# Gate and up products with the tokens as stationary operand, their result turned by block transposes and DMAs of quarters

## The chip, the cores and the metric

The kernel runs on one core of a Trainium2 chip. The core has a matrix engine (TensorE, PE in the profile; its loads of the stationary operand are PEld), a vector engine (VectorE, DVE), a scalar engine (ScalarE, ACT), a general engine (GpSimd, POOL) and a queue engine (SyncE, SP) that issues DMAs. Each engine works through its own list of instructions in order and waits on semaphores for the others. The metric is the device time of one execution in microseconds (us), as the median of several.

## The reference

The reference is two transformer blocks over 256 tokens of width 2048 in fp32. The first is a sliding-window attention block with attention sinks. The second has two attention branches (latent attention and differential attention), merged by gates, and then a feed-forward part. Only the feed-forward part and the last norm are touched here:

```
x  = x + merged @ w_out
h2 = rmsnorm(x, ffn_norm_g)
x  = x + (silu(h2 @ w_ffn_gate) * (h2 @ w_ffn_up)) @ w_ffn_down      # D_FF = 5632
return rmsnorm(x, final_norm_g)
```

## The kernel before

**Weights.** All weight matrices are cut into tiles of 128 x 128 and laid out in the order in which the kernel uses them: 5440 tiles in 340 *chunks* of 16 tiles (1 MB each). Class `Weights` streams them. `load` (L53) issues one DMA on SP for a chunk into one of four buffers `w_raw`. `cut` (L84, L85) splits half a chunk (8 tiles) into a high part `w_hi`, rounded on ScalarE, and a low part `w_lo`, the remainder on VectorE; four buffers each, so two chunks in split form. `take` hands out the tiles. Activations are split in the same way, and a product is hi*hi + hi*lo + lo*hi, accumulated in fp32 in PSUM.

**Two forms of matmul.** In `gemm` (L319, through `run`, L296) the weight tile is stationary and the tokens stream past: for each tile one matmul of 512 columns (the tokens' high and low parts side by side) and one of 256 columns. The result has features in the partitions and tokens along the free axis, which is the form that the next matrix needs as input. In `gemm_nat` (L375, through `nat3`, L367) the tokens are stationary, two blocks of 128, and four weight tiles side by side stream past: for each of the two blocks three matmuls of 512 columns. The result has tokens in the partitions. `down` uses `gemm_nat` (L989), gate and up use `gemm` (L963, L966; `gemm4` for the first two pairs).

**Feed-forward.** Gate and up are 1408 tiles, chunks 208 to 295; down is chunks 296 to 339. For each of 44 blocks of 128 features (L958 to L971) a gate and an up product are made; `total` (L389, L201) adds the two halves of a PSUM bank, `scaled` multiplies by the broadcast row `rb` of the norm's factor, Silu is applied (L965), the two are multiplied, and `split_scaled` (L234, L235) writes the split result `act`, which down takes. The residual `x2` lies with features in the partitions; the generator `after_out` (L939), of which `Interleave` puts one step among the matmuls after every 16 tiles, turns it with 32 transposes on TensorE (L949) and copies them out (L952) as `x2n`, tokens in the partitions, for the last residual addition (`residual`, L981).

**Order.** The program is written in Python in one order; a scheduler then sets the order of each engine's list, by its own estimate of when operands are ready, and every engine keeps to that list. A DMA of SP also waits, beside its data, for the eighth DMA before it on SP: eight semaphores are used in turn. A load of chunk c waits until chunk c - 4 is split, and a split of a half waits until the half four before it has been used by TensorE.

Of the kernel before, what the change touches and what calls it, by code (L numbers as in the profile page):

```python
# [9 lines left out]
F32 = mybir.dt.float32  # L10
# [160 lines left out]
def block_kernel(ctx, tc, order, w, x01, xt, bc, fg, cst, out):  # L171
# [247 lines left out]
    def transposed(p, on_act=False):  # L419
# [7 lines left out]
        else:  # L427
            nc.vector.tensor_copy(out=pt, in_=ps[:, 0:384])
        return pt


# [494 lines left out]
    for m, ps in blocks("out", 0, 16, mg):  # L926
# [7 lines left out]
        sq.add(t)  # L934
    rb = unit("rb_3")[:, 0:S]
    r_3 = const.tile([P, 2], F32, name="r_3")
    x2n = []

    def after_out():  # L939
        yield  # L940
        nc.vector.tensor_copy(out=r_3, in_=rstd(sq.sums(), D))
        yield
        rows(r_3, rb)
        for cb in range(4):
            for tb in range(2):
                yield
                ps = bank("t")
# [4 lines left out]
                nc.scalar.copy(out=t, in_=ps)  # L952
# [105 lines left out]


def _columns(v):  # L1060
    return np.asarray(v, np.float32).reshape(-1, P).T


def _matrices(i):

    pairs = []
    for j in range(16):
# [7 lines left out]
    kpe = in_2[:, 1280:1344]  # L1075
    ffn = np.concatenate([i["w_ffn_gate_2"][0], i["w_ffn_up_2"][0]], axis=1)
    return {
# [13 lines left out]
        "ffn": ffn,  # L1091
        "down": i["w_ffn_down_2"][0],
    }
# [34 lines left out]
```

## Time and profile before

| | |
|---|---|
| median of 3 runs | 2022.9 us (2022.58 to 2024.06) |
| the profiled execution | 2023.11 us |
| its span, first to last instruction | 2021.3 us |
| instructions in the span | 28390 |
| moved by DMAs | 364.83 MB, mean 180 GB/s |
| gate and up on TensorE | 1278.9 to 1773.3 us of the span |
| down on TensorE | 1773.3 us to the end of the matmuls |

A profile gives, for each engine, the instructions with their start and length. The *page* sums them. *Groups* put instructions of one line, engine and shape together; *by tile* does so for those that touch one named buffer; *waits* says which engine waited for which instruction; the *chain that ended last* is followed back from the last instruction, each step to what released it; the *timeline* lists instructions by start; *windows* sum a stretch of time. L198 is the line of the matmul helper and L201 that of the two-operand VectorE helper, so these are told apart by their buffers.

### The profile page before, as it was taken

The numbers are of one execution on the slowest core, as the hardware profiler recorded it, in microseconds if no ns is written. First come the engines' busy times: TensorE is split into PE (matmuls) and PEld (weight loads), VectorE is DVE, ScalarE is ACT, GpSimd is POOL, SyncE is SP. The second block draws the span as 40 slices with busy tenths as digits, with TensorE's granted clock in tenths as the row PEclk, the third lists the DMA queues.
The fourth block names the chain that finished last, engine by engine and source line by source line (L and its number), as shares of the span: only waits on it lengthen the run. The fifth ranks groups of instructions, "written<-read, shape, count | busy, mean of one in ns | idle before, by whom it ended". The sixth has DMA issues, their size and how long they took to land.

```text
span 2021.3 us, 28390 instructions
## 1 busy us (share of the span) xinstructions
PE 2007.7 (99%) x11338; PEld 1744.3 (86%) x11338; DVE 1309.4 (65%) x2151; ACT 1074.6 (53%) x1821; POOL 18.4 (1%) x25
## 2 busy tenths in 40 slices
PE   9999999999999999999999999999999999999998
PEld 8888888888888888888888888888888888888887
DVE  7778766887857555576665667656666666554544
ACT  6677665756546444455565445554444445444443
POOL 0000000000000000000000000000000000000000
PEclk9999999999999999999999999999999999999999
DMA  8444454444344555545445555455555555555553
GB/s 300 152 144 149 165 209 176 167 149 155 135 169 167 188 188 188 190 167 186 172 166 188 192 196 190 175 179 187 189 188 189 192 191 191 194 209 189 196 197 104
DMA packets 53235, 364.83 MB, mean 180 GB/s; under 512 B 6064, under 2 KB 6576, under 8 KB 9968
## 3 DMA queue, kind: packets, MB, share of 16 engines
q1 hardware_dynamic: 51552, 359.76, 49.8%
q10 hardware_dynamic: 1152, 1.97, 0.3%
q8 instruction: 88, 1.44, 0.3%
q0 software_dynamic: 400, 1.31, 0.2%
q14 instruction: 43, 0.35, 0.1%
HBM read 360.91 MB, written 2.10 MB: 180 GB/s over the span
## 4 chain that ended last, share of the span: by engine, by line
PE 96%; DVE 2%; ACT 1%; issue 1%; DMA 0%; POOL 0%; POOLq 0%; ACTq 0%
PE ps_g L198 88%; PE ps_s L198 5%; PE ps_t L198 2%; PE ps_t L423 1%; DVE rope_t L201 1%; DVE w_lo L85 0%; DVE k_n L201 0%; DVE q_r L201 0%; ACT w_hi L84 0%; DMA x01t<-x 0%; PE ps_t L949 0%; PE ps_t L853 0%; ACT prob L414 0%; PE ps_t L829 0%; DVE prob L408 0%
## 5 line engine op out<-in xcount | busy, mean ns | idle before, releaser
L85 DVE TENSOR_TENSOR w_lo<-w_raw,w_hi 128x1024 fp32r<-128x1024 f32 (+1 forms) x677 | 824.9, 1220 | 296.7 <-ACT w_hi L84 276.3
L84 ACT CAST w_hi<-w_raw 128x1024 fp32r<-128x1024 f32 (+1 forms) x677 | 708.2, 1047 | 352.9 <-PE ps_g L198 269.5
L198 PE MATMUL ps_g<-h,w_hi 128*128 128x512 f32 x3048 | 742.1, 392 | 0.1
L198 PEld LDWEIGHTS ps_g<-h,w_hi 128*128 128x128 f32 x3048 | 558.4, 188 | 111.2 <-issue 3.5
L198 PEld LDWEIGHTS ps_g<-h,w_lo 128*128 128x128 f32 x3048 | 392.1, 191 | 17.8 <-issue 3.2
L198 PE MATMUL ps_g<-h,w_lo 128*128 128x256 f32 x3048 | 404.0, 284 | 0.0
L198 PE MATMUL ps_g<-w_hi,act 128*128 128x512 f32 x688 | 212.1, 389 | 0.0
L198 PEld LDWEIGHTS ps_g<-w_hi,act 128*128 128x128 f32 x688 | 129.1, 188 | 26.9
L389 ACT COPY ffn<-ps_g 128x256 f32<-128x256 f32 x86 | 31.8, 373 | 200.6 <-PE ps_g L198 200.6
L198 PE MATMUL ps_g<-w_lo,act 128*128 128x512 f32 x344 | 133.8, 389 | 0.0
L201 DVE TENSOR_TENSOR ffn<-ffn,ps_g 128x256 f32<-128x256 f32 x86 | 35.8, 420 | 143.9 <-ACT ffn L389 143.9
L198 PE MATMUL ps_g<-w_hi,h 128*128 128x512 f32 x256 | 79.5, 389 | 0.0
L198 PEld LDWEIGHTS ps_g<-w_lo,act 128*128 128x128 f32 x344 | 64.6, 188 | 13.3
L198 PE MATMUL ps_g<-y_m,w_hi 128*128 128x512 f32 x256 | 63.8, 391 | 0.0
L198 PE MATMUL ps_g<-y_d,w_hi 128*128 128x512 f32 x256 | 61.2, 391 | 0.0
L198 PE MATMUL ps_g<-g,w_hi 128*128 128x512 f32 (+1 forms) x240 | 57.8, 377 | 0.0
L198 PEld LDWEIGHTS ps_g<-w_hi,h 128*128 128x128 f32 x256 | 48.0, 188 | 10.0
L198 PE MATMUL ps_g<-mg,w_hi 128*128 128x512 f32 x224 | 56.0, 391 | 0.0
L198 PEld LDWEIGHTS ps_g<-y_m,w_hi 128*128 128x128 f32 x256 | 47.0, 188 | 9.1
L198 PEld LDWEIGHTS ps_g<-y_d,w_hi 128*128 128x128 f32 x256 | 47.0, 188 | 9.1
L198 PE MATMUL ps_g<-c,w_hi 128*128 128x512 f32 x208 | 53.0, 397 | 0.0
L198 PE MATMUL ps_g<-w_lo,h 128*128 128x512 f32 x128 | 49.8, 389 | 0.0
(255 smaller groups left out, 1899.4 us busy)
## 6 DMA issues: line engine op xcount, KB each, us to landing
w_raw<-w SPq DMA_DIRECT2D x337, 1024.0 KB, 4.8
w_raw<-w SPq DMA_DIRECT2D x5, 512.0 KB, 7.6
x_t<-xt SPq DMA_DIRECT2D x7, 256.0 KB, 7.4
fgt<-fg POOLq DMA_DIRECT2D x4, 256.0 KB, 5.5
out<-x2n SPq DMA_DIRECT2D x4, 256.0 KB, 3.1
out<-x2n ACTq DMA_DIRECT2D x4, 256.0 KB, 3.5
x01t<-x SPq DMA_DIRECT2D x1, 310.0 KB, 4.8
w_raw<-w ACTq DMA_DIRECT2D x1, 256.0 KB, 5.0
```

The costliest lines, as they stand in the source:

```text
L84: a = nc.scalar.copy(out=hi[:, q], in_=src[:, q])
L85: b = nc.vector.tensor_tensor(out=lo[:, q], in0=src[:, q], in1=hi.bitcast(F32)[:, q], op=ALU.subtract)
L198: nc.tensor.matmul(out=o, lhsT=a, rhs=b, start=start, stop=stop, skip_group_check=True)
L201: nc.vector.tensor_tensor(out=o, in0=a, in1=b, op=op)
L389: nc.scalar.copy(out=o, in_=ps[:, S:])
L423: nc.tensor.transpose(out=ps[:, j * P:j * P + P], in_=p[:, j * P:j * P + P], identity=ident)
```

## The change

Gate and up are computed with `gemm_nat`, in 11 *units* of 512 features: four chunks of gate, then four of up. Unit u takes chunks 208 + 8u to 215 + 8u. Tokens lie in the partitions of the result, so the norm's factor `r_3` is a scale of the Silu on ScalarE, which reads PSUM, and VectorE multiplies the up product in PSUM by it. The row `rb` and the broadcasts are gone.

Down needs the product with features in the partitions. A block transpose on VectorE turns each 32 x 32 block of the 128 x 512 product in its place; the blocks are then moved to their partitions by 16 DMAs on SP, each of 32 partitions x 128 elements (16 KB, a *quarter*). ScalarE and VectorE split the result. x2 takes the same way: 32 transposes of 128 x 128 on VectorE and 8 x 16 quarters in place of the 32 transposes on TensorE and the copies, and the generator makes one of its eight steps in every third chunk and no longer in every one. The features that come together in this way are not in their old order, so the columns of gate, up and down and the final gain are permuted on the host beforehand and the output's columns afterwards.

```diff
     def nat3(o, hl, tb, hi, lo, first, last):
-        xh = hl[:, tb * P:tb * P + P]
-        xl = hl[:, S + tb * P:S + tb * P + P]
+        if isinstance(hl, list):
+            xh, xl = hl[tb]
+        else:
+            xh = hl[:, tb * P:tb * P + P]
+            xl = hl[:, S + tb * P:S + tb * P + P]
...
+    def moved(tr, name):
+        o = unit(name)
+        for a in range(4):
+            for b in range(4):
+                nc.sync.dma_start(out=o[32 * b:32 * b + 32, a * P:a * P + P],
+                                  in_=tr[32 * a:32 * a + 32, b * P:b * P + P])
+        return o
...
     def after_out():
         yield
         nc.vector.tensor_copy(out=r_3, in_=rstd(sq.sums(), D))
-        yield
-        rows(r_3, rb)
         for cb in range(4):
             for tb in range(2):
-                yield
-                ps = bank("t")
+                yield 3
+                tr = unit("x2_t")
                 for i in range(4):
-                    nc.tensor.transpose(out=ps[:, i * P:i * P + P], in_=x2[4 * cb + i][:, tb * P:tb * P + P],
-                                        identity=ident)
-                t = unit("x2n")
-                nc.scalar.copy(out=t, in_=ps)
-                x2n.append(t)
+                    nc.vector.transpose(
+                        out=tr.rearrange("p (a m j) -> p a m j", a=4, m=4)[:, :, i, :],
+                        in_=x2[4 * cb + i][:, tb * P:tb * P + P].rearrange("p (a j) -> p a j", a=4))
+                x2n.append(moved(tr, "x2n"))
...
-    for m in range(0, KF):
-        if m == 0:
-            b4 = gemm4("ffn", [0, KF, 1, KF + 1], h)
-        t = unit("ffn")
-        zg, zu = t[:, 0:S], t[:, S:]
-        ps = b4[2 * m] if m < 2 else gemm("ffn", m, h)
-        scaled(zg, ps, rb)
-        nc.scalar.activation(out=zg, in_=zg, func=AF.Silu)
-        ps = b4[2 * m + 1] if m < 2 else gemm("ffn", KF + m, h)
-        total(zu, ps)
-        tt(zu, zu, zg, ALU.mult)
-        hl = unit(f"act{m}", F32R)
-        split_scaled(zu, None, hl)
-        act.append(hl)
+    def hidden(pg, pu):
+        parts = []
+        for tb in range(2):
+            z = unit("ffn")
+            nc.scalar.activation(out=z, in_=pg[tb], func=AF.Silu, scale=r_3[:, tb:tb + 1])
+            parts.append(z)
+        yield
+        hls = []
+        for tb in range(2):
+            z = parts[tb]
+            tt(z, pu[tb], z, ALU.mult)
+            tr = unit("ffn_t")
+            nc.vector.transpose(out=tr, in_=z)
+            t = moved(tr, "ffn_m").rearrange("p (a g i) -> p g a i", a=4, g=4)
+            hi, lo = unit("act_hi", F32R), unit("act_lo", F32R)
+            nc.scalar.copy(out=hi.rearrange("p (g a i) -> p g a i", a=4, g=4), in_=t)
+            tt(lo.rearrange("p (g a i) -> p g a i", a=4, g=4), t,
+               hi.bitcast(F32).rearrange("p (g a i) -> p g a i", a=4, g=4), ALU.subtract)
+            hls.append((hi, lo))
...
+    for u in range(DFF // 512):
+        banks = []
+        work = hidden(gemm_nat("ffn", u * 512, h), banks)
+        next(work)
+        banks.extend(gemm_nat("ffn", DFF + u * 512, h))
+        for _ in work:
+            pass
```

The lists of the engines are the same as before up to the first matmul of gate. Three places in the feed-forward show what then moves. In the lists of the changed program L439 is a quarter, L958 a block transpose of x2, L972 the Silu, L980 the block transpose of a product and L983 the cast of `act_hi`; numbers behind a name tell buffers apart.

**SP, where unit 2 ends.** Before, the list from the last of the small loads to the end of the kernel:

```order
L460 DMA sinks<-bc 128x32
L53 DMA w_raw<-w 128x2048 x3
L461 DMA tab_a<-cst 128x384
L53 DMA w_raw<-w 128x2048 x333
L1033 DMA out<-x2n 128x512 x4
```

Now, from the load of chunk 231, the last of unit 2 (`w_raw_13363`), over those of chunks 232 and 233 to that of 234:

```order
L53 DMA w_raw_13363<-w 128x2048
L439 DMA x2n_13092<-x2_t_13087 32x128 x16
L439 DMA x2n_13216<-x2_t_13211 32x128 x16
L439 DMA x2n_13346<-x2_t_13341 32x128 x16
L439 DMA ffn_m_13400<-ffn_t_13398 32x128 x16
L53 DMA w_raw_13447<-w 128x2048
L53 DMA w_raw_13481<-w 128x2048
L439 DMA ffn_m_13424<-ffn_t_13422 32x128 x16
L53 DMA w_raw_13537<-w 128x2048
```

SP had nothing but loads for 333 DMAs; now 64 quarters stand between the loads of chunks 231 and 232, the last 16 of them those of unit 2's first product. In units 3 to 10 the quarters stand further back: behind the load of the fifth chunk after the unit's last, 16 of them, then two loads, then 16 more.

**VectorE, at the same place.** Before, ten rows from the feed-forward, where splits of weights (L85) and work on the products take turns:

```order
L85 TENSOR_TENSOR w_lo_13392<-w_raw_13389,w_hi_13391 128x1024
L201 TENSOR_TENSOR ffn_13243<-ffn_13243,ps_g_13291 128x256
L201 TENSOR_TENSOR ffn_13243<-ffn_13243 128x256
L85 TENSOR_TENSOR w_lo_13396<-w_raw_13389,w_hi_13395 128x1024
L235 TENSOR_TENSOR act9_13337<-ffn_13243,act9_13337 128x256
L85 TENSOR_TENSOR w_lo_13442<-w_raw_13439,w_hi_13441 128x1024
L201 TENSOR_TENSOR ffn_13340<-ffn_13340,ps_g_13341 128x256
L201 TENSOR_TENSOR ffn_13340<-ffn_13340,rb_3_12298 128x256
L85 TENSOR_TENSOR w_lo_13446<-w_raw_13439,w_hi_13445 128x1024
L85 TENSOR_TENSOR w_lo_13489<-w_raw_13486,w_hi_13488 128x1024
```

Now, from the split of chunk 231's second half (`w_lo_13382`) to that of chunk 232's first (`w_lo_13450`):

```order
L85 TENSOR_TENSOR w_lo_13382<-w_raw_13363,w_hi_13381 128x1024
L958 STREAM_TRANSPOSE x2_t_13341<-y_2857 128x4x32 x2
L958 STREAM_TRANSPOSE x2_t_13341<-y_2858 128x4x32 x2
L201 TENSOR_TENSOR ffn_13233<-ps_g_13237,ffn_13233 128x512
L201 TENSOR_TENSOR ffn_13235<-ps_g_13238,ffn_13235 128x512
L980 STREAM_TRANSPOSE ffn_t_13398<-ffn_13233 128x512
L201 TENSOR_TENSOR act_lo_13418<-ffn_m_13400,act_hi_13417 128x512
L980 STREAM_TRANSPOSE ffn_t_13422<-ffn_13235 128x512
L85 TENSOR_TENSOR w_lo_13450<-w_raw_13447,w_hi_13449 128x1024
```

Unit 2's products, both transpositions and the subtraction, which needs all sixteen quarters of `ffn_m_13400`, now stand ahead of the first split of chunk 232. In units 3 to 10 the splits of the next chunk and of half of the one after stand ahead of the unit's products, and five more halves ahead of the subtraction.

**ScalarE, in unit 3.** Before, nine rows of the feed-forward:

```order
L84 CAST w_hi_13635<-w_raw_13633 128x1024
L389 COPY ffn_13534<-ps_g_13535 128x256
L84 CAST w_hi_13639<-w_raw_13633 128x1024
L965 ACTIVATE ffn_13534<-ffn_13534 128x256
L84 CAST w_hi_13682<-w_raw_13680 128x1024
L389 COPY ffn_13534<-ps_g_13582 128x256
L84 CAST w_hi_13686<-w_raw_13680 128x1024
L234 CAST act12_13628<-ffn_13534 128x256
L84 CAST w_hi_13732<-w_raw_13730 128x1024
```

Now, from chunk 235, the last of unit 3's gate (`w_raw_13571`), to chunk 236, the first of its up (`w_raw_13611`):

```order
L84 CAST w_hi_13573<-w_raw_13571 128x1024
L84 CAST w_hi_13589<-w_raw_13571 128x1024
L972 ACTIVATE ffn_13605<-ps_g_13445,r_3_12298 128x512
L972 ACTIVATE ffn_13607<-ps_g_13446,r_3_12298 128x512
L84 CAST w_hi_13613<-w_raw_13611 128x1024
L84 CAST w_hi_13629<-w_raw_13611 128x1024
```

Unit 3's two Silus, which need its whole gate product, stand ahead of the first cast of chunk 236.

More of the change, by code (lines that the diff above doesn't have):

```diff
@@ L934, in block_kernel @@
         sq.add(t)
-    rb = unit("rb_3")[:, 0:S]
     r_3 = const.tile([P, 2], F32, name="r_3")
@@ L957, in block_kernel @@
     act = []
-    for m in range(0, KF):
-        if m == 0:
-            b4 = gemm4("ffn", [0, KF, 1, KF + 1], h)
-        t = unit("ffn")
-        zg, zu = t[:, 0:S], t[:, S:]
-        ps = b4[2 * m] if m < 2 else gemm("ffn", m, h)
-        scaled(zg, ps, rb)
-        nc.scalar.activation(out=zg, in_=zg, func=AF.Silu)
-        ps = b4[2 * m + 1] if m < 2 else gemm("ffn", KF + m, h)
-        total(zu, ps)
-        tt(zu, zu, zg, ALU.mult)
-        hl = unit(f"act{m}", F32R)
-        split_scaled(zu, None, hl)
-        act.append(hl)
+    def hidden(pg, pu):
[17 more added lines that the diff above has]
+            hls.append((hi, lo))
+        for k in range(4):
+            q = slice(k * P, k * P + P)
+            act.append([(hi[:, q], lo[:, q]) for hi, lo in hls])
+    for u in range(DFF // 512):
[5 more added lines that the diff above has]
+            pass
     between.drain()
@@ L1057, in _constants, with _quarters @@
     return c
+def _quarters(n):
+    return np.arange(n).reshape(-1, 4, 4, 32).transpose(0, 2, 1, 3).reshape(-1)
 def _columns(v):
@@ L1075, in _matrices @@
     kpe = in_2[:, 1280:1344]
-    ffn = np.concatenate([i["w_ffn_gate_2"][0], i["w_ffn_up_2"][0]], axis=1)
+    ffn = np.concatenate([i["w_ffn_gate_2"][0], i["w_ffn_up_2"][0]], axis=1)[:, _quarters(2 * DFF)]
     return {
@@ L1091, in _matrices @@
         "ffn": ffn,
-        "down": i["w_ffn_down_2"][0],
+        "down": i["w_ffn_down_2"][0][:, _quarters(D)],
     }
@@ L1109 @@
             "sinks_a", "lambda_q1_2", "lambda_q2_2", "lambda_k1_2", "lambda_k2_2")])[None], (P, 1)),
-        "fg": np.tile(i["final_norm_g_2"].reshape(1, D), (P, 1)),
+        "fg": np.tile(i["final_norm_g_2"][_quarters(D)].reshape(1, D), (P, 1)),
         "cst": _constants(),
@@ L1126 @@
     res = _run(nc, [arrays], core_ids=[0])
-    return res.results[0]["out"].reshape(1, S, D)
+    out = np.empty((1, S, D), np.float32)
+    out[0][:, _quarters(D)] = res.results[0]["out"].reshape(S, D)
+    return out
```

## The prediction

> **What bounds the kernel now.** The page comes first: which engine is busy, and whether its clock is whole.
>
> ```profile
> PE 2007.7 (99%) x11338; PEld 1744.3 (86%) x11338; DVE 1309.4 (65%) x2151; ACT 1074.6 (53%) x1821; POOL 18.4 (1%) x25
> PEclk9999999999999999999999999999999999999999
> PE 96%; DVE 2%; ACT 1%; issue 1%; DMA 0%; POOL 0%; POOLq 0%; ACTq 0%
> ```
>
> TensorE has no gaps, and the chain that ended last runs through it. So the kernel is as long as its row of matmuls, and a change acts by shortening that row or by tearing a hole in it. How near a hole is shows in the DMA queue's own waits, here from 1273 to 1773 us (us in total, times, longest):
>
> ```profile
> SPq L53 <- DVE w_lo L85: 249.1, 48, 6.0
> ```
>
> SP spends half of the stage waiting for the splits to free a weight buffer: loads run ahead, and no hole is near. Then the row itself, by the timeline (start, length): the first matmul of gate and up, two neighbouring blocks in the middle, the first matmul of down.
>
> ```profile
> 1278.91 0.61 PE L198 MATMUL ps_g<-h,w_hi 128*128 128x512 f32 x2
> ...
> 1441.12 2.08 PE L198 MATMUL ps_g<-h,w_lo 128*128 128x256 f32 x16
> ...
> 1446.69 2.08 PE L198 MATMUL ps_g<-h,w_lo 128*128 128x256 f32 x16
> ...
> 1773.31 0.39 PE L198 MATMUL ps_g<-w_hi,act 128*128 128x512 f32 x1
> ```
>
> The stage lasts 1773.31 - 1278.91 = 494.4 us for 88 chunks; one chunk (16 tiles) takes 5.57.
>
> **The change: what TensorE saves.** Down already works with tokens stationary, so its rows (count, duration in ns, first and last start) price the new form.
>
> ```profile
> L198 PE MATMUL ps_g<-w_hi,act x688: 389/389/389, 1773.3 to 2007.0; 128*128 128x512 f32 x172
> L198 PE MATMUL ps_g<-w_lo,act x344: 389/389/389, 1773.5 to 2006.8; 128*128 128x512 f32 x172
> ```
>
> 1032 matmuls start within 233.7 us: 0.2267 us apart, though each is drawn 389 ns long. A chunk in the new form is 24 of them, 5.44 us. 88 x 24 = 2112 take 478.8 us, and four small matmuls of the sums stay (0.4). The stage falls from 494.4 to 479.2: **-15.2 us**. Of that, 88 x (5.57 - 5.44) = 11.4 are the chunks; 3.4 are x2's transposes, since by the chain the blocks around each of the eight groups of four lie 6.00 apart and not 5.57:
>
> ```profile
> 1306.96 5.57 PE ps_g L198 x32
> 1312.96 5.57 PE ps_g L198 x32
> ```
>
> The rest is the broadcast of r_3. What ScalarE and VectorE lose in evacuations is worth nothing; they weren't the bound.
>
> **What it adds, and its prices.** VectorE's products, block transpositions and splits, and 480 quarters (DMAs of 16 KB) on SP, the queue that loads the weights. Nearest rows for 128x512 out of PSUM (ScalarE, VectorE), within SBUF, for 128x128, and for a half chunk's two split steps:
>
> ```profile
> L952 ACT COPY x2n<-ps_t x8: 578/587/588, 1303.3 to 1343.0; 128x512 f32<-128x512 f32 x8
> L983 DVE SCALAR_TENSOR_TENSOR x2n<-ps_g,r,x2n x7: 741/744/750, 1832.9 to 2007.4; 128x512 f32<-128x512 f32 x7
> L201 DVE TENSOR_TENSOR x2n<-x2n,fgt x6: 684/685/686, 1835.6 to 1955.9; 128x512 f32<-128x512 f32 x6
> L1029 DVE TENSOR_SCALAR x2n<-x2n,rstd x2: 486/488/489, 2009.8 to 2015.1; 128x512 f32<-128x512 f32 x2
> L286 DVE TENSOR_SCALAR diag<-ident,r x4: 278/280/286, 405.6 to 1292.1; 128x128 f32<-128x128 f32 x4
> L85 DVE TENSOR_TENSOR w_lo<-w_raw,w_hi 128x1024 fp32r<-128x1024 f32 x176 | 215.6, 1225 | 40.1 <-ACT w_hi L84 33.6
> L84 ACT CAST w_hi<-w_raw 128x1024 fp32r<-128x1024 f32 x176 | 185.3, 1053 | 37.9 <-PE ps_g L198 13.3 <-PE ps_s L198 13.1 <-issue 1.0
> ```
>
> Silu 0.6, product 0.75, cast 0.6, subtraction 0.68. No block transposition is in this trace: between 0.49 (one source, 128x512) and 1.23 (twice as wide); I take 0.68, and the ends move the sum by -0.4 and +1.3. A small one: 0.28.
>
> The quarters' price decides. SP's timeline at the start, and DMAs by size with us to landing:
>
> ```profile
> 0.74 0.39 SPq L209 DMA_DIRECT2D x01t<-x  x1
> 1.19 0.42 SPq L53 DMA_DIRECT2D w_raw<-w  x1
> ...
> 3.07 0.66 SPq L53 DMA_DIRECT2D w_raw<-w  x1
> ...
> 5.75 0.33 SPq L53 DMA_DIRECT2D w_raw<-w  x1
> 6.12 0.57 SPq L213 DMA_DIRECT2D x_t<-xt  x1
> ```
>
> ```profile
> w_raw<-w SPq DMA_DIRECT2D x337, 1024.0 KB, 4.8
> rope<-cst ACTq DMA_DIRECT2D x1, 256.0 KB, 2.7
> ```
>
> An issue costs 0.33 us whatever it carries, and the next follows at 0.37 (5.75 to 6.12); the busiest stretch has 0.45 and 0.66. A quarter: 0.37, or 5.9 us for sixteen. Landing: below rope's 2.7, so 2.4. Eight may be under way (each waits for the eighth before it), 2.4 / 8 = 0.30, so issuing binds. The Trainium skill ("DMA: Bandwidth & Descriptors", section "Bandwidth") speaks against such transfers: batch to 1 MiB or more, since those under 64 KB are bound by descriptors. Its fixed cost of about 2.0 us (section "Anatomy of one DMA") would, eight deep, be 0.25 a quarter and by that alone about 2026 us in the sum below; the issue row says 0.33 at least.
>
> **Where the quarters open holes.** SP, VectorE and ScalarE each work in order, so a quarter that waits for its transposition holds the loads behind it, and the subtraction that waits for its quarters holds the splits behind it. In units 3 to 10 VectorE has split three halves ahead when a unit ends, and loads up to five chunks beyond it stand ahead of the quarters. The load behind the first sixteen goes 2.2 + 5.9 = 8.1 us after the unit's end, lands at 12.9, and TensorE gets there at 27.2 (five chunks): covered. Without that cover each unit would pay; it would take about 0.7 us a quarter. VectorE has time: in a unit 16 splits of 1.23, two products, two transpositions and two subtractions are 23.9 of 43.5 us, and x2's 32 small transpositions are 9 us once. The permuted columns of gate, up, down and the final gain are laid out before the launch and cost nothing on the chip. Three places have no cover:
>
> *Chunk 223.* From the end of unit 0 on TensorE: two products and a transposition 2.2; sixteen quarters, 8.1; last landing 2.0, cast, subtraction, second transposition, 12.1; sixteen quarters and 0.8 behind load 220 in the ring of eight, 18.8; landing, cast, subtraction, four small transpositions, 23.2; 32 quarters of x2, 35.4 with some tenths between them; load 223 4.8, 40.2; cast and subtraction (the first matmul needs only the cast), 42.3. TensorE has seven chunks, 38.1. Hole: 4.3.
>
> *Chunk 232.* Its load and both splits stand behind unit 2's first transposition, product and sixteen quarters, and no half of it is split ahead. From the end of chunk 231: 2.2 + 5.9 + 4.8 + 2.05 = **15.0**, all of it hole. The 48 quarters of x2 ahead of it take 17.8 of about 19.8 us that SP has there; a dearer quarter overruns that too.
>
> *Chunk 236.* ScalarE has unit 3's two Silus, which wait for its gate, ahead of this chunk's cast: 2 x 0.6 + 1.05 + 1.0 = 3.3.
>
> Holes: 22.6 us. A long one also costs clock. The end of the kernel shows it: its last matmul by the timeline, then two stretches of 1 us, whose last three columns are granted clock, DMA share and GB/s.
>
> ```profile
> 2012.86 0.28 PE L198 MATMUL ps_s<-w_hi,act 128*128 128x256 f32 x1
> ```
>
> ```profile
> 2016.00:2017.00 1.00, 0.00 (x0) 0.00 (x0) 0.21 (x1) 0.40 (x1) 0.00 (x0) 0.96 0.59 227
> 2017.00:2018.00 1.00, 0.00 (x0) 0.00 (x0) 0.00 (x0) 0.00 (x0) 0.00 (x0) 0.50 1.13 356
> ```
>
> The last matmul ends at 2013.14, and at 2016.9, after 3.8 us, the clock halves. How soon it recovers no row shows: at once, or after another 3.8 at half pace, 1.9 lost. I take 1.9, for the hole at chunk 232. The Trainium skill ("TensorE: Matmul & The Clock Gate", section "Part 1: The HAM clock gate") has it return after about 3.4 us of work: by that 1.7.
>
> Sum: -15.2 + 22.6 + 1.9 = +9.3. The profiled execution took 2023.11 us (span 2021.3), 0.2 above the median of 2022.9: 2032.4, or 2032 from the median.
>
> **Rivals.** *Cheap quarters.* If SP issues small DMAs below 0.30 us and they land sooner, chunk 223 is covered, and 232 costs 9.1 + 16 x 0.30 = 13.9; with 3.3 and 1.9 less 15.2 that is +3.9, within 0.2% (4 us, about what a measurement can tell). At nearly nothing it is 9.1 + 3.3 + 1.9 - 15.2 = -0.9: 2022, not slower. For it: a quarter touches 32 partitions, a load 128. Against it: no issue in the trace is below 0.33.
>
> *Dear quarters.* At 0.46, as in the start's busy stretch, chunk 223 misses some 9, chunk 232 15.0 + 1.4 + 2.3 (48 quarters overrun by 2.3): with 3.3 about 31, and 2041. At 0.52 some 2050, at 0.66 about 2075. A landing of over 3 us acts alike, since eight are under way. For it: each quarter waits on a semaphore, which few loads of before had to. Against it: a quiet queue gave 0.37.
>
> *Columns alone.* The stationary load could hide entirely. The end's blocks of 256 columns come three in 0.36 us:
>
> ```profile
> 2012.38 0.28 PE L198 MATMUL ps_s<-w_lo,act 128*128 128x256 f32 x1
> ...
> 2012.74 0.28 PE L198 MATMUL ps_s<-w_lo,act 128*128 128x256 f32 x1
> ```
>
> So 256 more columns cost 0.2267 - 0.12 = 0.1067; 512 alone would be 0.2133, 28 us less over 2112: 2004, faster. The Trainium skill gives 215.7 ns for 512 (same page, "Back-to-back issue gap"), which would make it 2009. Against it: down has the same operands' form and runs at 0.2267.
>
> **How the numbers follow.** Forecast (0.30 to 0.46 a quarter, 2027 to 2041) 0.64; cheap 0.16; dear 0.17; columns alone, or a gain overlooked, 0.03. Slower is the forecast and the dear case, less a little at their lower edge: 0.80; within 0.2%: 0.17; faster: 0.03. The range goes from nearly free quarters, 2021, to 0.52 a quarter, 2050; 0.66 and the columns are left out.
>
> **What would show it.** In the changed profile: matmuls of gate and up 0.227 apart; no TensorE idle in units 3 to 10; three holes in TensorE's row, about 82, 135 and 172 us into the stage (before its 16th, 25th and 29th chunk), of 4, 15 and 3 us, the first two ended by the split of a load that came late; SP's quarters 0.37 apart; the clock at 0.50 for a few us. Wrong it would be if the big hole is under 10 us, if units 3 to 10 wait, or if the matmuls' spacing differs from down's.

## The result, and the profile after

The changed kernel takes 2070.35 us (median of 4 runs, 2069.75 to 2070.71) against 2022.88 for the kernel before (4 runs beside them): 1.0233 times as long, with a 95% interval of 1.0216 to 1.0251. It is slower, as forecast, but by 47 us and not by 9: well above 2050, where the forecast's range ended.

The page of the changed kernel, whose span is 2068.3 us against 2021.3 before: TensorE's and VectorE's busy time, the busy tenths of TensorE and its granted clock in 40 slices, the chain that ended last, and the DMAs by size with the us from issue to landing.

```profile
PE 2001.0 (97%) x10600; PEld 1705.5 (82%) x10600; DVE 1265.4 (61%) x2026; ACT 1034.5 (50%) x1681; POOL 18.4 (1%) x25
...
PE   9999999999999999999999999976699999999998
...
PEclk9999999999999999999999999988799999999999
...
PE 89%; SPq 5%; DVE 3%; DMA 2%; ACT 1%; issue 1%; POOL 0%; POOLq 0%; ACTq 0%
...
w_raw<-w SPq DMA_DIRECT2D x337, 1024.0 KB, 4.8
ffn_m<-ffn_t SPq DMA_DIRECT2D x352, 16.0 KB, 1.8
...
x2n<-x_t SPq DMA_DIRECT2D x128, 16.0 KB, 1.8
```

TensorE has fewer instructions and less work than before, and holes in three slices out of 40. SP's own issuing, which was not in the chain before, is now 5% of it, and the quarters land in 1.8 us. So the loss is in one place, near the beginning of the feed-forward. TensorE's timeline shows it (start, length, and in brackets the idle time before and what ended it), and further on the matmuls' spacing:

```profile
1379.89 1.22 PE L198 MATMUL ps_g<-w_hi,h 128*128 128x512 f32 x2 [12.76 <-ACT w_hi L84]
...
1383.61 0.62 PE L198 MATMUL ps_g<-w_hi,h 128*128 128x512 f32 x2
...
1463.39 1.22 PE L198 MATMUL ps_g<-w_hi,h 128*128 128x512 f32 x2 [31.70 <-ACT w_hi L84]
...
1491.55 0.73 PE L198 MATMUL ps_g<-w_hi,h 128*128 128x512 f32 x2 [1.77 <-ACT w_hi L84]
...
1769.78 0.62 PE L198 MATMUL ps_g<-w_hi,h 128*128 128x512 f32 x2
...
1788.14 0.62 PE L198 MATMUL ps_g<-w_hi,h 128*128 128x512 f32 x2
```

The three large holes stand before chunks 223, 232 and 236, where the prediction put them, but they are 12.8, 31.7 and 2.3 us (1.77, and another 0.53 before the first use of the chunk's low part `w_lo`) and not 4.3, 15.0 and 3.3. Between 1769.78 and 1788.14 lie 81 matmuls: 0.2267 us apart, as taken from down. By stretches (busy time and instructions of TensorE, its weight loads, VectorE, ScalarE, GpSimd; then granted clock, DMA share, GB/s):

```profile
1425.00:1450.00 25.00, 6.69 (x30) 5.21 (x28) 2.65 (x7) 0.00 (x0) 0.00 (x0) 0.69 0.10 26
1450.00:1475.00 25.00, 11.57 (x39) 8.93 (x40) 7.41 (x11) 5.23 (x6) 0.00 (x0) 0.63 0.37 130
1500.00:1525.00 25.00, 25.00 (x112) 20.67 (x112) 12.72 (x12) 10.02 (x10) 0.00 (x0) 1.00 0.47 172
1700.00:1725.00 25.00, 25.00 (x112) 20.71 (x111) 13.39 (x13) 11.78 (x13) 0.00 (x0) 1.00 0.59 223
```

In the large hole the computing engines all stand, at a DMA share of 0.10, while SP issues. The two later stretches, like all from 1500 us to the stage's end, show TensorE without a gap. Now SP, the queue of loads and quarters, over the same time:

```profile
1416.80 30.27 SPq L439 DMA_DIRECT2D x2n<-x_t  x48
1447.18 10.02 SPq L439 DMA_DIRECT2D ffn_m<-ffn_t  x16
1457.30 1.00 SPq L53 DMA_DIRECT2D w_raw<-w  x2
```

This is the cause of the 31.7 us as far as a trace can tell it: 48 quarters of x2 keep SP for 30.27 us, then unit 2's first sixteen for 10.02, and only then, at 1457.30, comes the load of chunk 232. Two rows of VectorE (transposition, subtraction) say which of the two groups of quarters, x2's or unit 2's own, was the worse:

```profile
1432.41 0.70 DVE L980 STREAM_TRANSPOSE ffn_t<-ffn 128x512 f32<-128x512 f32 x1
1459.08 0.69 DVE L201 TENSOR_TENSOR act_lo<-ffn_m,act_hi 128x512 fp32r<-128x512 f32 x1 [25.97 <-ACT act_hi L983]
```

Unit 2's product was turned at 1433.1; its quarters started 14 us later, when x2's had been issued. The price itself, by tile (count, duration in ns, first and last start):

```profile
L439 SPq DMA_DIRECT2D ffn_m<-ffn_t x352: 507/588/1705, 1324.3 to 1846.1; - x176
...
L980 DVE STREAM_TRANSPOSE ffn_t<-ffn x22: 699/702/705, 1323.6 to 1835.8; 128x512 f32<-128x512 f32 x22
```

An issue takes 0.588 us in the median, and 30.27 / 48 = 0.63 from start to start: not 0.37.

### The profile page after: what moved, and what is told of

It is laid out like the page before. It is cut to its first block, busy times and chain, and to the rows that moved or that the text cites. A ratio compares the mean times of both kernels' runs of the same rounds, so it can differ in the third digit from the quotient of the medians.

```text
span 2068.3 us, 27400 instructions
## 1 busy us (share of the span) xinstructions
PE 2001.0 (97%) x10600; PEld 1705.5 (82%) x10600; DVE 1265.4 (61%) x2026; ACT 1034.5 (50%) x1681; POOL 18.4 (1%) x25
## 4 chain that ended last, share of the span: by engine, by line
PE 89%; SPq 5%; DVE 3%; DMA 2%; ACT 1%; issue 1%; POOL 0%; POOLq 0%; ACTq 0%
PE ps_g L198 82%; SPq L439 5%; PE ps_s L198 4%; PE ps_t L198 2%; DMA w_raw<-w 1%; PE ps_t L426 1%; DVE w_lo L85 1%; DVE rope_t L201 1%; ACT w_hi L84 0%; DMA ffn_m<-ffn_t 0%; DVE k_n L201 0%; DVE q_r L201 0%; PE ps_t L865 0%; DVE act_lo L201 0%; ACT act_hi L983 0%
## 5 line engine op out<-in xcount | busy, mean ns | idle before, releaser
L85 DVE TENSOR_TENSOR w_lo<-w_raw,w_hi 128x1024 fp32r<-128x1024 f32 (+1 forms) x677 | 822.4, 1218 | 474.0 <-ACT w_hi L84 459.8
L198 PE MATMUL ps_g<-w_hi,h 128*128 128x512 f32 x1664 | 519.1, 392 | 49.4 <-ACT w_hi L84 49.4
L198 PE MATMUL ps_g<-h,w_hi 128*128 128x512 f32 x1672 | 410.3, 393 | 1.0 <-ACT w_hi L84 0.6
L198 PEld LDWEIGHTS ps_g<-w_hi,h 128*128 128x128 f32 x1664 | 314.3, 189 | 117.3 <-ACT w_hi L84 52.3
L198 PEld LDWEIGHTS ps_g<-h,w_hi 128*128 128x128 f32 x1672 | 306.1, 188 | 63.7 <-issue 3.5
L198 PE MATMUL ps_g<-w_lo,h 128*128 128x512 f32 x832 | 326.9, 393 | 3.4 <-DVE w_lo L85 3.3
L198 PE MATMUL ps_g<-h,w_lo 128*128 128x256 f32 x1672 | 223.2, 284 | 0.0
L198 PEld LDWEIGHTS ps_g<-h,w_lo 128*128 128x128 f32 x1672 | 214.3, 191 | 10.5 <-issue 3.2
L198 PEld LDWEIGHTS ps_g<-w_lo,h 128*128 128x128 f32 x832 | 157.5, 189 | 39.8 <-DVE w_lo L85 7.3
L198 PE MATMUL ps_g<-w_hi,act_hi 128*128 128x512 f32 x344 | 133.8, 389 | 0.0
L198 PE MATMUL ps_g<-w_lo,act_hi 128*128 128x512 f32 x344 | 133.8, 389 | 0.0
```

The costliest lines, as they stand in the source:

```text
L85: b = nc.vector.tensor_tensor(out=lo[:, q], in0=src[:, q], in1=hi.bitcast(F32)[:, q], op=ALU.subtract)
L198: nc.tensor.matmul(out=o, lhsT=a, rhs=b, start=start, stop=stop, skip_group_check=True)
```

## The experiments

The kernels ask four things: whether it is SP's list, what a quarter costs, what the parts do by themselves, and how much cover a move has. Spans are of the profiled execution; price_of_issue is read by its rows alone and left out of the table.

| kernel | median us | ratio to before (95%) | span us |
|---|---|---|---|
| changed kernel | 2070.35 | 1.0233 (1.0216 to 1.0251) | 2068.3 |
| x2_on_tensore | 2012.70 | 0.9945 (0.9930 to 0.9960) | 2009.7 |
| x2_spread | 2053.24 | 1.0141 (1.0125 to 1.0158) | 2053.2 |
| quarters_on_gpsimd | 2031.21 | 1.0038 (1.0025 to 1.0051) | 2029.4 |
| x2_by_gpsimd | 2009.06 | 0.9929 (0.9914 to 0.9944) | 2007.3 |
| five_dmas_by_dram | 2007.84 | 0.9924 (0.9909 to 0.9939) | 2005.9 |
| x2_alone | 2021.36 | 0.9992 (0.9982 to 1.0001) | 2020.7 |
| all_on_tensore | 2022.73 | 0.9997 (0.9988 to 1.0007) | 2020.6 |
| moves_of_20 | 2054.28 | 1.0158 (1.0141 to 1.0175) | 2050.6 |
| moves_of_24 | 2115.99 | 1.0447 (1.0429 to 1.0465) | 2115.0 |
| moves_of_32 | 2224.05 | 1.0993 (1.0977 to 1.1009) | 2223.3 |
| quarters_from_dram | 2052.25 | 1.0143 (1.0128 to 1.0158) | 2050.8 |

**Is it SP's list?** Two rivals were set against it: the latency of a move (product, transposition, quarters, cast, subtraction), and the amount of work added (data, transpositions, the new matmuls).

*x2_on_tensore* takes x2's 128 quarters away:

```
-                yield 3
-                tr = unit("x2_t")
...
-                x2n.append(moved(tr, "x2n"))
+                yield
+                ps = bank("t")
...
+                    nc.tensor.transpose(out=ps[:, i * P:i * P + P], in_=x2[4 * cb + i][:, tb * P:tb * P + P],
+                                        identity=ident)
+                t = unit("x2n")
+                nc.scalar.copy(out=t, in_=ps)
```

> The changed kernel with x2 turned on TensorE again (32 transposes, ScalarE copies, as before), so that its 128 quarters leave SP's list; the product's 352 quarters stay there. Theory (crowding): SP issues a quarter every 0.64 us, and the two long holes of 12.8 and 31.7 us are made by x2's 128 quarters (128 x 0.64 = 82 us of SP within the first three units) standing ahead of the loads. Then both holes go, units 0 to 10 are covered as units 3 to 10 are, and of the 15.2 us of gain 3.4 are given back: about 2011, up to 2015 with the small holes left. Rival (latency): what holds TensorE is the way product, transposition, quarters, cast, subtraction in front of the splits, however many quarters SP has; then a hole of 10 us or more stays before chunk 232, and the time is 2025 to 2045.

It took 2012.7, and TensorE is never idle in the stage (1278 to 1800, columns as above):

```profile
1278.00:1800.00 522.00, 522.00 (x2321) 432.35 (x2320) 273.94 (x262) 230.59 (x246) 2.88 (x5) 1.00 0.54 204
```

The theory's figure, and no hole, with the way from transposition to subtraction as long as ever (12.6 to 13.9 us, in units 3 to 10 of the changed kernel too). The 352 quarters of the product are carried; x2's 128 on top of them are not.

*x2_spread* keeps all 480 and spaces x2's steps:

```
-                yield 3
+                yield 10
```

> The changed kernel with all of its 480 quarters on SP, but a step of x2 every 10 chunks instead of every 3. Theory (crowding): a unit of 43.5 us then has 32 quarters of the product and about 13 of x2, 45 x 0.64 = 29 us of SP beside eight loads of 0.5: SP keeps up, the long holes go, and the whole gain of 15.2 shows, less small holes: 2008 to 2015. Rival (the quarters' own work, that is their data, VectorE's transpositions or the new matmuls): all of that is unchanged in amount, so the time stays near 2070.

It took 2053.2, which is neither the theory nor the rival. The long holes are gone (the longest is 5.2 us), but there are many. SP's timeline in the middle of the row says why:

```profile
1367.59 11.21 SPq L439 DMA_DIRECT2D ffn_m<-ffn_t  x16
1378.90 1.00 SPq L53 DMA_DIRECT2D w_raw<-w  x2
1382.21 11.00 SPq L439 DMA_DIRECT2D ffn_m<-ffn_t  x16
1393.31 1.00 SPq L53 DMA_DIRECT2D w_raw<-w  x2
1396.73 10.02 SPq L439 DMA_DIRECT2D x2n<-x_t  x16
1406.85 1.00 SPq L53 DMA_DIRECT2D w_raw<-w  x2
```

The list goes round in bundles: wait for a transposition, sixteen quarters, two loads, 14.5 us in all (1367.59 to 1382.21, and on to 1396.73). With three bundles SP delivers six loads in 43.5 us where TensorE uses eight. My sum of 29 us had counted the quarters and not the waits between them.

*quarters_on_gpsimd* issues them elsewhere:

```
-                nc.sync.dma_start(out=o[32 * b:32 * b + 32, a * P:a * P + P],
+                nc.gpsimd.dma_start(out=o[32 * b:32 * b + 32, a * P:a * P + P],
```

> The changed kernel with the 480 quarters issued by GpSimd's queue instead of SP's; nothing else. Theory (crowding of SP's list): loads no longer stand behind quarters; the splits still stand behind the subtractions that wait for quarters. If GpSimd issues at 0.7 us or less, the hole of 31.7 us falls under 10 and the time to 2008 to 2020; at 1 us or more, the 48 quarters of x2 and 16 of unit 2 take over 60 us there and the subtraction waits as before, 2040 to 2070. Rival (a 16 KB move costs the same wherever it is issued, or the DMA engines are the limit): as slow as the changed kernel, with landings far over 1.8 us.

GpSimd issues a quarter in 0.50 us, so by the expectation this should have been 2008 to 2020; it took 2031.2. With the quarters out of SP's list, and at that lower price, 39 us are gone against the changed kernel. By spans 23.5 us more than in the fastest kernel below, which has no hole, remain. Of these, 4.4 lie behind the last matmul, where GpSimd's own last step, a DRAIN, took 10.64 us and not 1.08. The others lie in the stage, where TensorE is idle for 12.1 us. No cast of weights waits for a load there; the waits from 1278 to 1800 us show for what instead (us in total, times, longest):

```profile
ACT act_hi L983 <- DMA ffn_m<-ffn_t: 113.0, 21, 11.1
DVE act_lo L201 <- ACT act_hi L983: 98.7, 21, 9.7
```

The splits of the weights stand behind subtractions that wait for quarters, and x2's quarters stand ahead of the product's on GpSimd's list too. A quarter also lands later, 3.9 us after its issue and not 1.8. So the loads behind quarters are the larger part, and the way through the quarters to the splits, the rival, is the smaller one; the sizes are rough, since price and landing changed with the queue.

**What does a quarter cost, and why?** *price_of_issue* is the kernel before with rows of DMAs behind its last output (x2n's last tile is the source):

```
+    for a, b in rc:
+        nc.sync.dma_start(out=d[0][32 * b:32 * b + 32, a * P:a * P + P], in_=s[32 * a:32 * a + 32, b * P:b * P + P])
...
+    for k in range(16):
+        nc.sync.dma_start(out=d[3][8 * k:8 * k + 8, :], in_=s[8 * k:8 * k + 8, :])
+    for a, b in rc:
+        nc.sync.dma_start(out=d[4][32 * b:32 * b + 32, a * P:a * P + P], in_=fg[32 * a:32 * a + 32, b * P:b * P + P])
+    for k in range(4):
+        nc.sync.dma_start(out=d[5], in_=fg[:, k * 512:k * 512 + 512])
+    for k in range(4):
+        nc.sync.dma_start(out=d[6], in_=s)
```

> The kernel before with rows of DMAs behind its last output, to price an issue where nothing else is under way; the output is the reference's. On SP: 16 of 32x128 within SBUF (the quarters' form), 8 of 128x128 and 8 of 32x512 within SBUF, 16 of 8x512 (16 KB too, some without a wait), 16 of 32x128 and 4 of 128x512 from DRAM, 4 of 128x512 within SBUF; then 16 quarters on ScalarE's queue and 16 on GpSimd's. Theory (form): the price comes with the form, 32 rows of 512 bytes, or with SBUF as source: then the quarters take 0.59 here too, 0.64 start to start, in quiet as in the stage, and one of the other forms with fewer rows or from DRAM takes 0.33 to 0.4. Rival (wait): the price is that of waiting on a semaphore at each issue; then the DMAs without a wait take 0.33 and those with one 0.5 or more, whatever their form. Rival (busy queue): it comes from other traffic in the stage; then quarters take about 0.37 here.

SP's timeline behind the outputs, where no load is under way (GpSimd issues its own sixteen quarters from 2016.68 to 2024.55, beside SP's first): quarters (L1042), 128x128 (L1044), 32x512 (L1046) and 8x512 (L1048) within SBUF; 32x128 (L1050) and 128x512 (L1052) from DRAM; 128x512 within SBUF (L1054).

```profile
2016.44 10.61 SPq L1042 DMA_DIRECT2D spare<-x2n  x16
2027.16 2.63 SPq L1044 DMA_DIRECT2D spare<-x2n  x4
...
2033.08 4.40 SPq L1046 DMA_DIRECT2D spare<-x2n  x7
2037.57 10.78 SPq L1048 DMA_DIRECT2D spare<-x2n  x16
2048.46 7.33 SPq L1050 DMA_DIRECT2D spare<-fg  x16
...
2064.95 0.33 SPq L1052 DMA_DIRECT2D spare<-fg  x1
2066.07 0.47 SPq L1054 DMA_DIRECT2D spare<-x2n  x1
```

A quarter takes 10.61 / 16 = 0.66 here too (0.59 in the median, one of 1.03), and 0.59 in the last three, issued after GpSimd's: so it isn't the traffic. The 8x512 took 0.624 at the least, and three of them, which have no wait in SP's list, 0.624 to 0.642: it isn't the wait. The same 32x128 from DRAM goes at 7.33 / 16 = 0.46, and 128x512 from DRAM, sixteen times its size, takes 0.33. A source in SBUF alone doesn't make it dear: a write of 128x512 out of SBUF into DRAM takes 0.34 (in *five_dmas_by_dram* below). So the price comes with both ends in SBUF, and there it is higher for fewer rows, whatever their length: in the median 0.62 for 8 rows, 0.57 to 0.59 for 32, 0.50 to 0.55 for 128. Why that is so, no run tells.

*quarters_from_dram* uses this: fifteen of sixteen quarters read the final gain in DRAM, so this kernel leaves the move itself out and keeps only its DMAs.

```
+                of = tr if a + b == 0 else fg
                 nc.sync.dma_start(out=o[32 * b:32 * b + 32, a * P:a * P + P],
-                                  in_=tr[32 * a:32 * a + 32, b * P:b * P + P])
+                                  in_=of[32 * a:32 * a + 32, b * P:b * P + P])
```

> The changed kernel, 480 quarters on SP as there, but of each move only the first quarter reads the turned unit; the other fifteen have the same form and read the final gain in DRAM (so the feed-forward's product and the residual are wrong). The quarters then cost 0.42 and 0.46 from start to start instead of 0.59 and 0.64; loads and bundles stand a little differently (five loads between x2's 48 quarters and unit 2's sixteen). Theory (issue price): 16 of them take 7.4 instead of 10.3 us, 48 take 22 instead of 31; of the 60 us of holes most go, 2008 to 2041 (2041 is the prediction's own sum at 0.46 in the changed kernel's order). Rival (number of DMAs or the waits on their landings, not their price at issue): 2060 or more.

2052.2, above the theory's end and below the rival's. Cheaper issue helps, by 18 us, but not enough in this list, where 48 of x2's quarters still stand in a row (the rows show the last two moves' fifteen and the loads behind them), and TensorE's timeline has the hole at the same place:

```profile
1417.35 7.07 SPq L440 DMA_DIRECT2D x2n<-fg  x15
...
1425.08 7.07 SPq L440 DMA_DIRECT2D x2n<-fg  x15
1432.25 8.77 SPq L53 DMA_DIRECT2D w_raw<-w  x5
```

```profile
1438.32 1.22 PE L198 MATMUL ps_g<-w_hi,h 128*128 128x512 f32 x2 [16.63 <-ACT w_hi L84]
```

The 48 stand from 1406.9 to 1432.2, 25 us without a load; the load at 1432.25 ends the hole. TensorE's row over the stage:

```profile
1278.00:1800.00 522.00, 490.90 (x2112) 400.68 (x2112) 257.70 (x274) 209.02 (x220) 2.88 (x5) 0.97 0.53 192
```

TensorE is idle for 522.00 - 490.90 = 31.1 us, and 31 is what the prediction's own steps add up to at 0.46 (in the changed kernel's order), where its sum said 2041. So price times number in a row gives the holes; the other 11 us are matmuls at less than full pace after them.

**Taking the issues away, not the moves.** *five_dmas_by_dram*:

```
-        for a in range(4):
-            for b in range(4):
-                nc.sync.dma_start(out=o[32 * b:32 * b + 32, a * P:a * P + P],
-                                  in_=tr[32 * a:32 * a + 32, b * P:b * P + P])
+        o, d = unit(name), dram.tile([P, 512], F32, name="turned", tag="turned", bufs=8)
+        nc.sync.dma_start(out=d, in_=tr)
+        for b in range(4):
+            nc.sync.dma_start(out=o[32 * b:32 * b + 32, :].rearrange("p (a j) -> p a j", a=4),
+                              in_=d.rearrange("(a p) (b j) -> b p a j", a=4, b=4)[b])
```

> The changed kernel with each move of sixteen quarters replaced by five DMAs on SP: the turned unit is written to DRAM whole, and four DMAs read it back with the quarters in their places. The same 30 moves at the same places of the program, x2's every 3 chunks as in the changed kernel. Theory (SP's issue time): a move costs SP 0.5 + 4 x 0.42 = 2.2 us instead of 10.3, so loads are never late: 2008 to 2015, although each move now takes two landings one behind the other, some 2 us longer. Rival (latency of the move, for which the subtractions and behind them the splits wait): the holes stay or grow, 2060 or more.

2007.84, the fastest of all. One move in SP's timeline (write, a load that now fits between, four reads):

```profile
1415.47 0.34 SPq L438 DMA_DIRECT2D turned<-ffn_t  x1
1415.91 0.38 SPq L53 DMA_DIRECT2D w_raw<-w  x1
1417.61 1.74 SPq L440 DMA_DIRECT2D ffn_m<-turned  x4
```

A move costs SP 2.1 us and takes two landings (2.0 and 4.3 us by the page, a quarter's is 1.8), with twice the data; TensorE is never idle in the stage. Data and landings, then, are not what costs. The move as a whole is shorter all the same, about 8 us against 12, since 10 of the 12 were issuing; and the loads stand elsewhere in the list, between write and reads. So this run alone doesn't part the loads' share from the splits' share; quarters_on_gpsimd does that, roughly.

*x2_by_gpsimd* leaves the product's quarters on SP and gives x2's to GpSimd, every 10 chunks:

```
-                yield 3
+                yield 10
...
-                x2n.append(moved(tr, "x2n"))
+                x2n.append(moved(tr, "x2n", nc.gpsimd))
```

> The changed kernel with x2's 128 quarters on GpSimd's queue and a step of x2 every 10 chunks; the product's 352 quarters stay on SP. Theory (SP's list goes round in bundles: wait for a transposition, sixteen quarters at 0.64, two loads; three bundles a unit of 43.5 us are too many, two are not): SP's list is as when x2 is on TensorE, no hole opens, and x2's transposes are saved as well: 2007 to 2010, a little under x2_on_tensore. Rival (VectorE's list: x2's transpositions and the subtractions that wait for quarters hold the splits wherever the quarters are issued): holes as with all quarters on GpSimd, 2020 or more.

2009.06, no idle TensorE: two bundles a unit on SP are carried, and x2's transposes are saved as well.

**The parts by themselves.** *x2_alone* is the kernel before with the change's part for x2:

```
-                    nc.tensor.transpose(out=ps[:, i * P:i * P + P], in_=x2[4 * cb + i][:, tb * P:tb * P + P],
...
+                    nc.vector.transpose(
...
+                x2n.append(moved(tr, "x2n"))
```

> The kernel before with only x2 turned the new way (VectorE's transpositions, 128 quarters on SP, a step every 3 chunks; columns of down and the final gain permuted); gate and up stay as they were. Theory (bundles): a bundle of sixteen, 10.3 us, and three loads, 1.5, go into 3 chunks of 16.7 us, so one bundle per three chunks is carried by itself, and the 3.4 us of x2's transposes show: 2019 to 2023. Rival (x2's quarters alone make the holes): a hole of over 10 us in the first 30 chunks, 2030 or more.

2021.36: within the theory's range. Its ratio's interval, 0.9982 to 1.0001, doesn't tell it from no change; one hole of 1.5 us, at 1426, took part of the 3.4. No hole of 10 us opens: x2's quarters alone are carried.

*all_on_tensore* has the new form of gate and up and turns everything on TensorE:

```
-            tr = unit("ffn_t")
-            nc.vector.transpose(out=tr, in_=z)
...
+            for k in range(4):
+                nc.tensor.transpose(out=ps[:, k * P:k * P + P], in_=z[:, k * P:k * P + P], identity=ident)
```

> The changed kernel with nothing turned by VectorE and no quarters: x2 as before, and the product by 88 transposes on TensorE. Theory: gate and up in the new form save 11.8 us, 88 transposes cost 88 / 32 x 3.4 = 9.4: 2020 to 2021. Were the new form of the matmuls itself what costs the time, it would be 2040 or more.

2022.73, some 2 us above the expectation: by spans the 88 transposes cost 2020.6 - 2009.7 = 10.9 against x2_on_tensore, not 9.4, and eat the gain of 11.6 up. The form of the matmuls isn't what costs.

**How much cover does a move have?** In *moves_of_24*, *moves_of_32* and *moves_of_20* some or all of the product's quarters are cut in two, with x2 on TensorE (the diff is that of 24; with 32 parts is always 2, with 20 the condition is b < 1):

```
+                parts = 2 if b < 2 else 1
+                n = P // parts
+                for j in range(parts):
+                    nc.sync.dma_start(out=o[32 * b:32 * b + 32, a * P + j * n:a * P + j * n + n],
+                                      in_=tr[32 * a:32 * a + 32, b * P + j * n:b * P + j * n + n])
```

> x2_on_tensore with half of the product's quarters cut in two (32x64), so that a move is 24 DMAs on SP and not 16; nothing else. It tests how much cover units 3 to 10 have; the prediction put the end of the cover at about 0.7 us a quarter, that is 11 us for a move. Theory (bundles): per unit SP needs two bundles of a wait of 3.3, 24 x 0.64 = 15.4 and two loads, 1.0, so 39.4 us, and four loads more, 2: 41 of 43.5 us. It just fits: 2012 to 2020. Rival (the prediction's figure, that a move of over 11 us opens a hole in each unit by what it is longer, since the first load behind it is late): 4 us a unit, ten units, 2050.

> x2_on_tensore with every quarter of the product cut in two: 32 DMAs a move. Theory (bundles): two bundles of 3.3 + 20.5 + 1.0 and four loads more are 51.6 us a unit against TensorE's 43.5: 8 us a unit, ten or eleven units, 2012.7 + 80 to 90 = 2090 to 2105. By the prediction's figure, 20.5 - 11 = 9.5 a move that opens the unit, 2105. If SP's issue time were not the limit, but the landing or the data, which are unchanged: 2013.

24 DMAs a move took 2116, far above both figures; 32 took 2224, above the 2105. By spans each DMA added cost 105.3 / (22 x 8) = 0.60 and 213.6 / (22 x 16) = 0.61 us, which looks like its whole price at issue, but it is a sum of two things. TensorE from 1278 to 2030, with 20, 24 and 32 DMAs a move:

```profile
1278.00:2030.00 752.00, 725.37 (x3156) 592.29 (x3155) 364.78 (x347) 305.46 (x327) 2.88 (x5) 0.99 0.50 188
1278.00:2030.00 752.00, 684.68 (x2872) 552.77 (x2871) 333.17 (x316) 279.30 (x299) 2.88 (x5) 0.95 0.46 175
1278.00:2030.00 752.00, 588.53 (x2395) 467.93 (x2394) 278.74 (x268) 233.92 (x252) 2.88 (x5) 0.88 0.39 147
```

TensorE is idle for 26.6, 67.3 and 163.5 us, while the spans are 40.9, 105.3 and 213.6 longer than that of x2_on_tensore; the rest is matmuls at less than full pace, at granted clocks of 0.99, 0.95 and 0.88. VectorE's rows in one move of moves_of_24 (transposition, subtraction, the next splits):

```profile
1698.56 0.70 DVE L984 STREAM_TRANSPOSE ffn_t<-ffn 128x512 f32<-128x512 f32 x1
...
1717.54 0.69 DVE L201 TENSOR_TENSOR act_lo<-ffn_m,act_hi 128x512 fp32r<-128x512 f32 x1 [6.39 <-ACT act_hi L987]
...
1722.09 2.36 DVE L85 TENSOR_TENSOR w_lo<-w_raw,w_hi 128x1024 fp32r<-128x1024 f32 x2 [3.24 <-ACT w_hi L84]
```

Between transposition and subtraction stand six splits here, three chunks or 16.3 us of TensorE's; the way takes 19.0 (1698.56 to 1717.54), and the next splits come later still, since their load stood behind the 24 as well. In x2_on_tensore five splits stand there, 13.6 us, the way takes 13.6 (1632.06 to 1645.64), and the subtraction waits 1.1 us:

```profile
1632.06 0.70 DVE L981 STREAM_TRANSPOSE ffn_t<-ffn 128x512 f32<-128x512 f32 x1
...
1645.64 0.69 DVE L201 TENSOR_TENSOR act_lo<-ffn_m,act_hi 128x512 fp32r<-128x512 f32 x1 [1.10 <-ACT act_hi L984]
```

Sixteen quarters fit. But the number of DMAs is not all that differs. In x2_on_tensore five splits stand on that way in every move but the first; with 20, 24 and 32 DMAs it is four to seven, from move to move, and after the first units SP has five and seven loads between two units in turn where it had six. So the scheduler's order of the lists changed along with the number. The last run asked where the edge is:

> x2_on_tensore with a quarter of the product's quarters cut in two: 20 DMAs a move, 22 moves. The spans of moves_of_24 and moves_of_32 lie 105.3 and 213.6 us above x2_on_tensore, 0.60 and 0.61 for each DMA added, as if no cover were left beyond sixteen. Theory (the cover of a move ends at about 16 quarters at 0.64, 10.3 us, in both moves of a unit): 4 x 22 x 0.6 = 53, so 2062 to 2066. Rival (the prediction's 0.7 a quarter, 11.2 us, or 17.5 DMAs): 2.5 x 22 x 0.6 = 33, so 2045. Rival (the loss at 24 comes from another order of the list, and the bundles of a unit fit into it until they fill it): 2013 to 2020.

2054.3, between the first two cases. The way from transposition to subtraction is 15.2 to 17.8 us there (22.8 to 24.0 with 32). TensorE's four long holes in gate and up, 3.4 to 3.6 us, lie some 97 us apart, one in every second unit; the others are under 2 us. So the cover ends between 16 and 20 DMAs, between 10.0 and 12.5 us of issuing. How much of the loss beyond it is the DMAs' own and how much is the other order of the lists, which was a rival, these runs don't part.

## Why the prediction was wrong

The direction and the places were right; the size was wrong, mostly by one term, which the prediction put as "A quarter: 0.37, or 5.9 us for sixteen". The runs show 0.63 from start to start in the stage, 10.0 us for sixteen, and nearly the same in a quiet queue. A second term, the clock, was too small as well: 1.9 us against 9.6.

- *TensorE's gain, -15.2:* right. Without holes (five_dmas_by_dram) the span falls from 2021.3 to 2005.9, by 15.4; with x2 left on TensorE by 11.6, against 11.8 worked out.
- *The issue price, 0.37:* wrong. It was read from a load out of DRAM and extended to "whatever it carries". The rows of before held no DMA within SBUF, so the row was near in size of instruction and far in kind; the rows of 0.45 and 0.66 that stood beside it were taken for a busy stretch, and of the two rows that gave the 0.37 it used the length of the first alone: the second, at 6.12, took 0.57.
- *Landing 2.4, block transposition 0.68, product, cast, subtraction:* 1.8, 0.70, 0.69 (two in 1.37), 0.62 and 0.69. None matters here.
- *Units 3 to 10 covered up to about 0.7 us a quarter:* not contradicted. 0.63 in the changed kernel opens no hole from 1500 us on, and moves of 20 DMAs, 12.5 us or 0.78 for sixteen, do; the edge lies between, and the runs beyond it differ in the order of the lists too. The loss of moves_of_24, 9.6 us a unit by spans, was well above the 4 that I expected by this figure.
- *Three holes, 22.6 us:* the places were right. With 0.63 in the same steps chunk 223 has 64 quarters that take 0.26 longer, 4.3 + 16.6 = 20.9 (measured 12.8, and 4.4 in smaller holes ahead of it); chunk 232 has 15.0 + 16 x 0.26 for its own, and 48 quarters that take 30.3 of 19.8 us, 29.7 (measured 31.7). Before chunk 236 ScalarE's two Silus (1489.14, 1.37 us) do stand ahead of the cast, and the hole is 2.3. With 3.3, 1.9 and -15.2 that is 2063.5. The holes add up to 53.9 with 0.63 and to 52.8 as measured, though each is off by 1 to 4 us, in both directions. So the steps were sound, and the "dear" rival, given a chance of 0.17, is what happened, though not for the reason that it gave, the wait on a semaphore; the range ended at 0.52 because "a quiet queue gave 0.37". That its 2075 at 0.66 lies near 2070 is luck: the same steps give about 2067 there, and 2063.5 at the 0.63 that was measured; what is missing to 2070 is the clock.
- *Clock, 1.9 us:* too small. The span is 62.4 longer than without holes; TensorE is idle for 522.00 - 469.17 = 52.8 of it:

```profile
1278.00:1800.00 522.00, 469.17 (x2031) 383.15 (x2031) 248.59 (x266) 200.74 (x211) 0.69 (x1) 0.95 0.48 181
```

The other 9.6 are time in which TensorE works at less than full pace. After the hole of 12.8 us eight matmuls take 3.7 us (1379.89 to 1383.61) and not 1.8: 1.9, as taken for one hole. After the 31.7 us eleven take 5.3 and not 2.5: 2.8. And after the third hole, of 1.77 and 0.53, eight take 3.4 (1492.81 to 1496.19): 1.6, at half the clock:

```profile
1493.00:1494.00 1.00, 1.00 (x3) 0.81 (x4) 0.92 (x2) 1.00 (x2) 0.00 (x0) 0.50 1.02 434
```

The prediction had read 3.8 us of idle time until the clock halves off the kernel's end, and charged one hole; here three holes cost clock, one of them with no idle time above 1.8 us. The remaining 3.3 us are spread over the edges of all twelve idle times and weren't taken apart. The Trainium skill ("TensorE: Matmul & The Clock Gate", section "Part 1: The HAM clock gate") gives about 3.4 us of work until the full clock is back: the first and the third hole agree with that, at 3.7 and 3.4, the second took longer.

Together: -15.4 + 52.8 + 9.6 = 47.0 = 2068.3 - 2021.3. The 9.6 is what is left of the 62.4 beside the idle time, and 1.9 + 2.8 + 1.6 = 6.3 of it were counted in rows.

## What to carry to other kernels

A DMA costs its queue an issue whose price depends on where it reads and writes, 0.59 us within SBUF and 0.42 from DRAM for the same 32x128: take it from a row of the same kind, and where there is none, keep the dearest issue in the trace inside the range. Many small moves on the queue of the loads cost number times price in one piece, and what stands behind them (here a load, and behind the subtraction the splits) has just the cover of the work queued ahead of it; count that cover in the list, move by move. Where a move within SBUF takes many DMAs, a round trip by DRAM in a few can be cheaper for the queue: 2.1 us instead of 10, and here 47 us slower became 15 us faster.

## What the runs showed of the hardware that was not expected

- The issue of a DMA on SP took 0.59 us for 16 KB within SBUF (32x128), 0.62 for 8x512, 0.55 to 0.57 for 64 KB, 0.47 to 0.54 for 128x512, but 0.42 for the 32x128 from DRAM and 0.33 to 0.42 for a 128x512 from DRAM or, at 0.34, out of SBUF into DRAM. ScalarE's queue took 0.60 for a quarter, GpSimd's 0.50.
- The waits on other DMAs cost nothing that shows: with or without one, 8x512 took 0.62 to 0.64, the first of the row (0.72) apart.
- VectorE's block transposition of 128x512 took 0.70 us, as a subtraction of that size does.
- The granted clock fell to 0.50 after idle times of 1.77 and 0.53 us with two matmuls between them, and stayed at 1.00 after 1.39 and 0.53. After holes of 12.8 and 31.7 us TensorE needed 3.7 and 5.3 us of work until its full pace.
- GpSimd's last DRAIN took 10.64 us in the run that had issued all 480 quarters on its queue, 1.66 with x2's 128 on it, and 1.08 with none of them.
